# A first stage in fixed order, and three re-timings further on, in a two-layer encoder on one Trainium2 core

## The chip, the core and the metric

The kernel runs on one core of one Trainium2 chip. The core has a matrix engine (TensorE, PE in the profile; its weight loads are shown apart as PEld), a vector engine (VectorE, DVE), an engine for functions of one input (ScalarE, ACT), a general engine (GpSimd, POOL) and an engine that here issues all transfers (SyncE, SP). Each engine works through a list of instructions in the order in which they stand there; a semaphore makes an instruction wait for another engine or for a transfer, and whatever stands behind it on the same engine waits too. The metric is the device time of one execution in microseconds (us); a lower time is better.

## What is computed

The reference is an encoder of two layers over one sequence of 1024 tokens of width 1024. All arithmetic is float32.

```python
c_act = silu(c)
for l in range(2):
    mod = c_act @ ada_w[l] + ada_b[l]
    shift, scale, gate = split(mod, 3)
    h = rms_norm(x, norm_g[l]) * (1 + scale) + shift
    y = even_mixer(h) if l == 0 else odd_mixer(h)
    x = x + gate * y
return rms_norm(x, final_g)
```

`rms_norm(x, g)` is x times rstd times g, with rstd = 1 / sqrt(mean(x*x) + 1e-6) for each token. The even mixer projects h to 3072 columns, then runs differential attention (4 heads, two softmax maps each, values of width 128) and beside it a gated linear recurrence (RG-LRU) over 512 channels; both are gated and go into one output projection. The odd mixer projects h to 4096 columns, runs neighbourhood attention (16 heads, window 8 x 16 on a 16 x 64 grid), gates it and projects it back.

## The kernel before

Activations are held transposed: channels on the 128 partitions (eight blocks k = 0 to 7), tokens along the row in two halves of 512 (hf = 0, 1). To keep float32 accuracy on PE, each operand is split into a high part (type fp32r, a rounded copy) and a low part (the rest), and a product is three matmuls: high by high, high by low, low by high. Weights come in slabs of 128 output columns (512 KB). For each, ACT copies the high part (`whi`, L185) and POOL subtracts for the low part (`wlo`, L186).

**Who sets the order.** The program is written as one trace of operations. A planner then orders each engine's list by its own estimate of times: it goes by the order of the trace, but may put an operation that it takes to be ready ahead of one that it takes to be waiting. `tc.high_priority()` moves a block forward in the planner's preference. `tc.issue_after(ins)` places the block's operations that run on the engine of `ins` behind `ins` in that engine's list. SP's list is planned in the same way.

**The first stage** (L503 to L608) makes h of the first layer and the first three slabs' projections (two for the recurrence, one for the values) at once, as the transfers arrive. For each half, the squares of x are made on ACT and DVE (`squares`), summed over channels on PE (`ss_add`, L368: 32 small matmuls that leave the sums of four token groups on 32 partitions each), turned into rstd on DVE by a bit trick and three Newton steps (`rstd_rows`, eleven instructions, L378 to L384), spread over the partitions by PE (`spread`, L397) and copied to SBUF by ACT (`bcs`, L545). The modulation is made in four groups g of two channel blocks (`mod_first`): eight pieces of `ada_w` are loaded, summed on PE (L273), copied as a row by ACT (`mrow`, L296), turned by a small matmul with `pick` (L298), and DVE adds the bias (L302) and makes the gain (L304). `make_h` (L404 to L406) then makes for each k and half: x times gain times rstd on DVE, the high part with the shift on ACT, the low part on DVE. `products(i, g, hf)` (L563 to L565) adds the six matmuls of group g, slab i and half hf to the slab's PSUM bank. The sums of groups 1 to 3 stand in `high_priority` blocks, and the planner puts them well ahead of the products that need them.

**Behind the stage** a `Feed` holds projections as jobs in pieces of six matmuls, each worth 1300 credits. In the first layer's attention, each of the four `step()` calls of a unit (128 queries of a head; 33 rounds) pumps PUMP credits of such filler between the attention's own instructions. At the boundary between the layers, `out_layer` runs the output projection, half by half, eight slabs each; between its slabs the modulation of the second layer is summed: `mod_part` loads eight pieces of `ada_w`, adds them up on DVE (L334, L336), lets `wait` further turns pass, and then sums over the partitions on PE (`mrow`, L368 and L353), behind the newest projection matmul (`state["pe"]`). `NW[2]` is the number of those turns there. In the second layer, `v1_job` makes values and writes them to DRAM in eight pieces (`vd<-vt`, L1196); `load_v` reads them back in another layout (`vc<-vd`, L1208) for the products with the attention weights (L1330).

## Time and profile before

| | |
|---|---|
| median of 3 runs | 1210.18 us (1206.6 to 1210.3) |
| profiled execution, its own time | 1210.03 us |
| span of that execution's instructions | 1208.0 us |
| PE busy | 1151.2 us (95% of the span) |
| DVE, ACT, POOL busy | 728.8, 566.6, 387.0 us |
| moved by DMA | 132.26 MB |

The span runs from the first instruction to the last; the profiled execution's own time has 2.0 us more around it. An engine is busy while it executes; L numbers are lines of the kernel. `pp<-ahi,whi` names what is written and what is read, by the program's names (`ahi`, `alo` are the split activations). In a timeline row stand the start, the duration, the engine, the line, the operation, the operands and how many instructions the row merges; the bracket gives the engine's idle time ahead of it and what ended it. In a row of waits stand the instruction that waited, what it waited for, the total, how often, and the longest. The granted clock is the share of full speed that TensorE's clock was given.

### The profile page before, as it was taken

To read this page: it belongs to the slowest core of one execution; us is meant where nothing else is said; L and a number is where in the kernel's file an instruction comes from. 1 tells how busy PE (TensorE), PEld (TensorE's weight loads), DVE (VectorE), ACT (ScalarE), POOL (GpSimd) and SP (SyncE) were. 2 spreads that over 40 slices of the span, in tenths; PEclk is the share of its full clock that TensorE was granted. 3 is DMA by queue.
4 is the path that set the end of the run, shared out by engine and by line. 5 is a ranking of instruction groups with operands and counts; after the bars stand their busy time and mean duration, and the time that the engine had idled before them with its cause. 6 is when DMAs were issued, how large, how long until landed. Compare 5 with 4: busy or idle time off the path is not lost.

```text
span 1208.0 us, 19169 instructions
## 1 busy us (share of the span) xinstructions
PE 1151.2 (95%) x7232; PEld 980.0 (81%) x7232; DVE 728.8 (60%) x1414; ACT 566.6 (47%) x1031; POOL 387.0 (32%) x354
## 2 busy tenths in 40 slices
PE   4999999999999999779999899999999999999996
PEld 3788778888778887657879788988998898888896
DVE  6757949588889889658873244333444434546354
ACT  4357586466555558423433344334444434445121
POOL 2124421332323344524423332332333333216200
PEclk8999999999999999889999999999999999999998
DMA  9723132322121110276523432343445444214212
GB/s 329 228 73 122 51 94 77 94 82 75 38 86 53 58 46 21 67 231 222 179 74 117 130 93 86 94 141 101 128 132 141 136 128 132 78 52 150 99 71 71
DMA packets 82045, 132.26 MB, mean 109 GB/s; under 512 B 7584, under 2 KB 48672, under 8 KB 81952
## 3 DMA queue, kind: packets, MB, share of 16 engines
q1 hardware_dynamic: 81952, 131.03, 34.8%
q8 instruction: 57, 0.93, 0.3%
q14 instruction: 36, 0.29, 0.1%
HBM read 110.03 MB, written 14.68 MB: 103 GB/s over the span
## 4 chain that ended last, share of the span: by engine, by line
PE 78%; DVE 9%; DMA 4%; issue 4%; ACT 3%; POOL 2%; SPq 0%; DVEq 0%; POOLq 0%; ACTq 0%
PE pp L201 16%; PE pp L202 16%; PE pp L203 15%; PE no L1330 3%; PE etr L1312 3%; PE v L201 2%; PE v L202 2%; PE v L203 2%; PE atr L957 2%; DMA vd<-vt 2%; PE s L659 2%; PE s L660 2%; PE n L659 2%; PE n L660 2%; DVE e L927 1%
## 5 line engine op out<-in xcount | busy, mean ns | idle before, releaser
L202 PE MATMUL pp<-alo,whi 128*128 128x512 f32 (+1 forms) x1040 | 395.0, 380 | 3.6 <-POOL alo L226 3.6
L201 PE MATMUL pp<-ahi,whi 128*128 128x512 f32 (+1 forms) x1040 | 397.2, 382 | 0.2 <-DVE ks L630 0.2
L203 PE MATMUL pp<-ahi,wlo 128*128 128x512 f32 (+1 forms) x1040 | 394.8, 380 | 1.0 <-POOL wlo L186 1.0
L186 POOL TENSOR_TENSOR wlo<-raw,whi 128x1024 fp32r<-128x1024 f32 x80 | 197.5, 2472 | 268.5 <-ACT whi L185 254.5
L202 PEld LDWEIGHTS pp<-alo,whi 128*128 128x128 f32 x1040 | 197.1, 189 | 37.6 <-POOL alo L226 4.3
L203 PEld LDWEIGHTS pp<-ahi,wlo 128*128 128x128 f32 x1040 | 196.7, 189 | 38.1 <-POOL wlo L186 1.8
L201 PEld LDWEIGHTS pp<-ahi,whi 128*128 128x128 f32 x1040 | 196.9, 189 | 35.7 <-issue 2.1
L1301 POOL TENSOR_SCALAR e<-e,r 128x288 f32<-128x288 f32 (+1 forms) x128 | 71.3, 570 | 239.7 <-DVE r L1299 239.3
L185 ACT ACTIVATE whi<-raw 128x1024 fp32r<-128x1024 f32 x80 | 84.3, 1056 | 121.0 <-PE pp L202 65.7
L1296 ACT ACTIVATE e<-e,nm 128x288 f32<-128x288 f32 (+1 forms) x128 | 72.7, 569 | 51.3 <-DVE nm L1293 50.7
L931 ACT ACTIVATE e<-e,nm 128x1024 f32<-128x1024 f32 x64 | 73.5, 1149 | 47.7 <-DVE nm L927 45.5
L1293 DVE CUSTOM_DVE_ANT_0 e<-n,bias 128x288 f32<-128x288 f32 (+1 forms) x128 | 60.4, 504 | 51.9 <-PE n L660 32.2
L1318 DVE COPY e<-etr 96x384 f32<-96x384 f32 (+1 forms) x64 | 35.5, 554 | 91.1 <-PE etr L1312 89.5
L1316 ACT ACTIVATE e<-etr 96x384 f32<-96x384 f32 (+1 forms) x64 | 31.3, 490 | 118.9 <-DVE e L1318 118.5
L927 DVE CUSTOM_DVE_ANT_0 e<-s,tb 128x1024 f32<-128x1024 f32 x64 | 77.1, 1219 | 10.1 <-PE s L660 9.1
L201 PE MATMUL v<-whi,ahi 128*128 128x256 f32 x256 | 72.2, 282 | 0.0
L203 PE MATMUL v<-whi,alo 128*128 128x256 f32 x256 | 71.9, 281 | 0.0
L202 PE MATMUL v<-wlo,ahi 128*128 128x256 f32 x256 | 71.9, 281 | 0.0
L948 POOL TENSOR_SCALAR e<-e,r 128x256 f32<-128x256 f32 x32 | 33.9, 1059 | 110.1 <-DVE r L937 47.2
L964 ACT ACTIVATE ath<-atr 128x512 fp32r<-128x512 f32 x64 | 37.7, 596 | 40.4 <-PE atr L957 40.0
L1062 DVE SCALAR_TENSOR_TENSOR xh<-pp,mod,xh 128x512 f32<-128x512 f32 (+1 forms) x40 | 25.7, 641 | 50.8 <-PE pp L203 49.9
L1067 ACT ACTIVATE sq<-xh 128x512 f32<-128x512 f32 (+1 forms) x40 | 21.7, 543 | 72.8 <-DVE xh L1062 71.9
(207 smaller groups left out, 2076.4 us busy)
## 6 DMA issues: line engine op xcount, KB each, us to landing
raw<-in_w_dram SPq DMA_DIRECT2D x56, 512.0 KB
ada<-in_adaw_dram SPq DMA_DIRECT2D x96, 256.0 KB
raw<-in_wo_dram SPq DMA_DIRECT2D x24, 512.0 KB
bias<-in_nab_dram SPq DMA_DIRECT2D x64, 144.0 KB
qq<-qq SPq DMA_DIRECT2D x48, 128.0 KB
bias<-in_nab_dram SPq DMA_DIRECT2D x32, 192.0 KB
xT<-in_xT_dram SPq DMA_DIRECT2D x16, 256.0 KB
xh<-in_xTp_dram SPq DMA_DIRECT2D x16, 256.0 KB
```

Source lines behind the costliest of these rows:

```text
L185: A.activation(hi[:], raw[:], AF.Copy)
L186: G.tensor_tensor(lo[:], raw[:], hi[:], ALU.subtract)
L201: T.matmul(ps, lh, rh, start=start, stop=False)
L202: T.matmul(ps, lh, rl, start=False, stop=False)
L203: state["pe"] = T.matmul(ps, ll, rh, start=False, stop=stop).ins
L659: T.matmul(dst, qsel(q[m]), k, start=True, stop=False)
L660: T.matmul(dst, qsel(q[2 + m]), k, start=False, stop=True)
L927: state["dve"] = V.tensor_tensor_reduce(out=e[:], in0=ps[:].rearrange("p a b -> p (a b)"), in1=tbt[h][:, o:o + S], scale=-1.0, scalar=3.0e ...
L931: A.activation(e[:], e[:], AF.Exp, scale=-1.0, bias=nm[:], accum_out=sums[:, m:m + 1])
L1293: state["dve"] = V.tensor_tensor_reduce(out=e[:, m, :n], in0=ps[:, m, :n], in1=bias["now"][m][:, :n], scale=-1.0, scalar=3.0e38, op0=ALU.a ...
L1296: A.activation(e[:, m, :n], e[:, m, :n], AF.Exp, scale=-1.0, bias=nm[:, m:m + 1], accum_out=sums[:, m:m + 1])
L1301: state["pool"] = G.tensor_scalar(e[:, m, :n], e[:, m, :n], r[:, m:m + 1], 0.0, ALU.mult, ALU.add).ins
```

## The change

- **First stage.** A class `Pinned` wraps an engine so that each instruction issued through it stays behind everything traced on that engine so far. All squares, sums, rstd, spreads, modulation and products of the first stage go through it: the order on DVE, ACT and PE is the order of the program. `mod_first` becomes a generator in five parts (loads; sums of five pieces; sums of three; row copy; pick, bias and gain).
- rstd is a root on ACT, a reciprocal on DVE and one Newton step; the spread rstd stays in PSUM. `scaled` multiplies x by it there, ahead of the modulation; `parts` then makes the high part on ACT as x * gain + shift, the same value `h` on DVE, and the low part as `h` less the high part.
- The small constants of the recurrence are traced behind the stage, and their first DVE and ACT instructions that need the lamp load, as well as the gate weights' splits on ACT, are placed behind the stage's last `parts`.
- `PUMP` is 745 instead of 800.
- `NW[2]` is 7 instead of 3, and the rest of the second layer's modulation is stepped in the first two slabs of the boundary's second half.
- `load_v` is placed behind the newest traced write of values on SP.

```diff
-NW = (3, 3, 3, 3)
+NW = (3, 3, 7, 3)
-PUMP = 800.0
+PUMP = 745.0
...
+    class Pinned:
+        def __init__(self, eng):
+            self.eng = eng
+        def __getattr__(self, name):
+            f = getattr(self.eng, name)
+            return lambda *a, **k: tc.keep_in_program_order(f(*a, **k))
...
     def mod_first(g, pool, small, c32, V, A, T):
         pieces = []
         for k in range(KC):
...
             pieces.append(piece)
+        yield
+        ps = ptp.tile([P, HF], F32, tag="pt", name=f"mod{g}")
+        for k in range(KC):
+            for n in range(4):
+                cols = pieces[k][:, n // 2, (n % 2) * P:(n % 2 + 1) * P]
+                T.matmul(ps[32 * n:32 * n + 32, :P], c32[:, k, :], cols, start=k == 0,
+                         stop=k == KC - 1)
+            if k == 4:
+                yield
+        yield
         row = pool.tile([P, P], F32, tag="mrow", name="mrow", bufs=2)
         A.activation(row[:], ps[:, :P], AF.Copy)
+        yield
         pc = ps[:, P:]
         T.matmul(pc[:, :4], row[:], pick[:], start=True, stop=True)
...
+        def rstd(hf):
+            v, rr, t = (stp.tile([P, P], F32, tag=g, name=g)[:] for g in ("rs", "rr", "rt"))
+            pA.activation(t, nbank[hf][:, :P], AF.Sqrt, bias=eps[:], scale=1.0 / D)
+            pV.tensor_scalar(v, nbank[hf][:, :P], 1.0 / D, EPS, ALU.mult, ALU.add)
+            pV.reciprocal(rr, t)
+            pV.scalar_tensor_tensor(t, rr, -0.5, rr, ALU.mult, ALU.mult)
+            pV.tensor_tensor(t, t, v, ALU.mult)
+            pV.scalar_tensor_tensor(rr, t, 1.5, rr, ALU.add, ALU.mult)
+            return rr
+        def scaled(k, hf):
+            pV.tensor_tensor(half(k, hf), half(k, hf), nbank[hf][:], ALU.mult)
+        def parts(k, hf):
+            g, b = first_mod[k]
...
+            state["first A"] = pA.activation(hi[:], half(k, hf), AF.Identity, scale=g, bias=b).ins
+            pV.tensor_scalar(h[:], half(k, hf), g, b, ALU.mult, ALU.add)
+            state["first V"] = pV.tensor_tensor(lo[:], h[:], hi[:], ALU.subtract).ins
...
+        load_x(0)
+        mod = [mod_first(g, adp, stp, c32, pV, pA, pT) for g in range(KC // 2)]
+        next(mod[0])
         slab(0)
+        for k in range(KC):
+            square(pV if k in (2, 5) else pA, k, 0)
         with tc.issue_after(state["ada"].ins):
+            load_x(1)
+        norm_sums(0, pp, "pp")
+        next(mod[0])
+        rr = rstd(0)
+        spread(rr, nbank[0], T=pT)
+        next(mod[0])
+        scaled(0, 0)
+        scaled(1, 0)
+        square(pV, 0, 1)
+        square(pV, 1, 1)
+        next(mod[0])
         slab(1)
         with tc.issue_after(state["x"].ins):
+            next(mod[1])
+        next(mod[0])
+        parts(0, 0)
+        parts(1, 0)
+        for k in range(2, KC):
+            square(pA, k, 1)
+        for k in range(2, 6):
+            scaled(k, 0)
         products(0, 0, 0)
         products(1, 0, 0)
+        norm_sums(1, ptp, "pt")
+        rr = rstd(1)
+        spread(rr, nbank[1], T=pT)
         slab(2)
+        scaled(6, 0)
...
+        for k in (0, 1):
+            scaled(k, 1)
+        for k in (0, 1):
+            parts(k, 1)
+        scaled(7, 0)
+        products(2, 0, 0)
+        products(1, 0, 1)
+        products(0, 0, 1)
+        scaled(2, 1)
+        scaled(3, 1)
         for g in range(1, KC // 2):
+            next(mod[g])
+            next(mod[g])
+            next(mod[g])
+            products(2, g - 1, 1)
+            next(mod[g])
...
             for hf in range(2):
+                for k in (2 * g, 2 * g + 1):
+                    parts(k, hf)
+            if g == 1:
+                for k in range(4, KC):
+                    scaled(k, 1)
             for i in range(2):
                 for hf in range(2):
                     products(i, g, hf)
+            products(2, g, 0)
...
+        products(2, KC // 2 - 1, 1)
         for hf in range(2):
             evac_v(0)(hf, banks[2, hf])
+        small_constants(stp)
...
-        some(mod, 99)
         t0 = tail(0, to_h1)
         for c in range(KC):
             some(r1, 1)
+            some(mod, (4, 99)[c] if c < 2 else 0)
             some(t0, (1, 1, 2, 2, 2, 2, 0, 0)[c])
...
-            nc.sync.dma_start(vt[:4 * w], vd4[:, y, P * p:P * p + P].rearrange("g y e -> y g e"))
+            with tc.issue_after(state["vd"]):
+                nc.sync.dma_start(vt[:4 * w],
+                                  vd4[:, y, P * p:P * p + P].rearrange("g y e -> y g e"))
```

More of the change, by code (lines that the diff above doesn't have):

```diff
@@ L264, with mod_first @@
     first_mod = {}
-    def mod_first(g, pool, small, c32):
-        ps = ptp.tile([P, HF], F32, tag="pt", name=f"mod{g}")
-        def sums(x, w, start, stop):
-            for n in range(4):
-                cols = x[:, n // 2, (n % 2) * P:(n % 2 + 1) * P]
-                state["modmm"] = T.matmul(ps[32 * n:32 * n + 32, :P], w, cols,
-                                          start=start, stop=stop)
+    def mod_first(g, pool, small, c32, V, A, T):
         pieces = []
@@ L284, in mod_first @@
             pieces.append(piece)
-        if g == 0:
-            for k in range(KC):
-                sums(pieces[k], c32[:, k, :], k == 0, k == KC - 1)
-        else:
-            with tc.high_priority():
-                sums(pieces[KC - 1], c32[:, KC - 1, :], True, False)
-                with tc.issue_after(state["modmm"].ins):
-                    for k in range(KC - 1):
-                        sums(pieces[k], c32[:, k, :], False, k == KC - 2)
+        yield
[8 more added lines that the diff above has]
+        yield
         row = pool.tile([P, P], F32, tag="mrow", name="mrow", bufs=2)
         A.activation(row[:], ps[:, :P], AF.Copy)
+        yield
         pc = ps[:, P:]
@@ L364, in ss_start, with ss_add @@
         return ptp.tile([P, HF], F32, tag="pt", name=name)
-    def ss_add(ss, sq, start, stop, w=P):
+    def ss_add(ss, sq, start, stop, w=P, T=T):
         for j in range(4):
@@ L519, in squares, with square, norm_sums @@
                                                                hf * HF:(hf + 1) * HF])
+        def square(eng, k, hf):
+            sq = sqs[k, hf] = stp.tile([P, HF], F32, tag="sq", name="sq", bufs=SQ)
+            if eng is pV:
+                pV.tensor_tensor(sq[:], half(k, hf), half(k, hf), ALU.mult)
+            else:
+                pA.activation(sq[:], half(k, hf), AF.Square)
+        def norm_sums(hf, pool, tag):
             ss = nbank[hf] = pool.tile([P, HF], F32, tag=tag, name=f"norm{hf}")
-            sqs = []
@@ L537 @@
-        bcs = {}
-        def scale(hf):
-            with tc.high_priority():
-                rr = rstd_rows(nbank[hf], D, stp)
-                spread(rr, nbank[hf])
-                bcs[hf] = stp.tile([P, HF], F32, tag="bcs", name="bcs")
-                A.activation(bcs[hf][:], nbank[hf][:], AF.Copy)
-        def parts(g, hf):
-            for k in (2 * g, 2 * g + 1):
-                make_h(0, k, hf, half(k, hf), bcs[hf][:])
+                ss_add(ss, sqs[k, hf], k == 0, k == KC - 1, T=pT)
@@ L562, in products @@
                 ps, (wh, wl), (hi, lo) = banks[i, hf], ready[i], hact[k, hf]
[L563 to L568 removed]
+                pT.matmul(ps, wh[:, k, :], hi[:], start=k == 0, stop=False)
+                pT.matmul(ps, wl[:, k, :], hi[:], start=False, stop=False)
@@ L577 @@
         products(0, 0, 0)
         products(1, 0, 0)
+        norm_sums(1, ptp, "pt")
+        rr = rstd(1)
+        spread(rr, nbank[1], T=pT)
         slab(2)
-        with tc.issue_after(state["modmm"].ins):
-            scale(1)
-        parts(0, 1)
-        with tc.issue_after(state["x"].ins):
-            mod_first(2, adp, stp, c32)
-        for i in range(2):
-            products(i, 0, 1)
-        rest = [(2, 0, 0), (2, 0, 1)]
-        for g in range(1, KC // 2):
+        scaled(6, 0)
+        with tc.issue_after(state["ada"].ins):
+            next(mod[2])
@@ L590 @@
+        for k in (0, 1):
[8 more added lines that the diff above has]
+        scaled(3, 1)
+        for g in range(1, KC // 2):
+            next(mod[g])
[3 more added lines that the diff above has]
+            next(mod[g])
             if g == 1:
-                with tc.issue_after(state["x"].ins):
-                    mod_first(3, adp, stp, c32)
+                with tc.issue_after(state["ada"].ins):
+                    next(mod[3])
@@ L597 @@
                     products(i, g, hf)
-            for args in rest:
-                products(*args)
-            rest = [(2, g, 0), (2, g, 1)]
+            products(2, g, 0)
         for i, evac in enumerate((evac_xb(0), evac_xb(1))):
@@ L603 @@
                 evac(hf, banks[i, hf])
-        for args in rest:
-            products(*args)
+        products(2, KC // 2 - 1, 1)
         for hf in range(2):
             evac_v(0)(hf, banks[2, hf])
+        small_constants(stp)
         ahead(3)
@@ L821 @@
         vj = lambda h: both(at0[c_v + h], evac_v(h))
-        gate_w(0)
-        gate_w(1)
+        with tc.issue_after(state["first A"]):
+            gate_w(0)
+            gate_w(1)
         kq0 = lambda: chain(both(at0[c_k], evac_k(("a", 0))), both(at0[c_q], evac_q(("a", 0))))
```

53 lines of the change are left out of this document (19 added, 34 removed).

## The prediction

> **What bounds the kernel now.** I read the page's busy line first, then the waits of TensorE (PE), then windows around each wait, and last the timeline of the first stage, whose every instruction is re-ordered.
>
> ```profile
> span 1208.0 us, 19169 instructions
> PE 1151.2 (95%) x7232; PEld 980.0 (81%) x7232; DVE 728.8 (60%) x1414; ACT 566.6 (47%) x1031; POOL 387.0 (32%) x354
> ```
>
> PE is idle for 56.8 us of the span; PE work itself hardly changes, so the change can only move idle time and half clock. The waits of PE, longest first (total, times, longest):
>
> ```profile
> PE norm L368 <- ACT sq L527: 7.9, 2, 6.9
> PE mrow L368 <- issue: 7.3, 1, 7.3
> PE start L563 <- ACT ahi L405: 6.1, 2, 4.1
> PE no L1330 <- DMA vc<-vd: 4.2, 3, 3.4
> PE pp L202 <- POOL alo L226: 3.6, 2, 3.2
> PE obc L397 <- DVE osq L384: 3.3, 2, 2.6
> ```
>
> Four places: the first stage (norm, start), the tail of the first layer's attention (alo, obc), the boundary between the layers (mrow), and the value loads of the second layer (vc). Windows around them (busy of PE, PEld, DVE, ACT, POOL, then granted clock, DMA share, GB/s):
>
> ```profile
> 39.00:75.00 36.00, 35.77 (x261) 28.92 (x262) 24.73 (x34) 16.73 (x25) 7.20 (x3) 0.95 0.38 120
> ...
> 228.00:464.00 236.00, 232.69 (x1392) 193.49 (x1391) 205.59 (x418) 141.28 (x248) 80.08 (x80) 1.00 0.20 62
> 464.00:516.00 52.00, 43.58 (x252) 35.65 (x251) 38.33 (x71) 30.00 (x45) 26.04 (x20) 0.90 0.13 41
> ...
> 527.00:542.00 15.00, 7.66 (x28) 5.53 (x27) 7.29 (x11) 2.59 (x4) 2.82 (x2) 0.66 0.89 296
> ...
> 682.00:692.00 10.00, 6.60 (x61) 5.52 (x60) 3.40 (x8) 3.13 (x6) 3.33 (x3) 0.83 0.61 179
> ```
>
> Two things to see. The late first stage (39 to 75) has only 0.2 us of idle PE. And a wait costs twice: at 682 to 692 PE idles 3.4 us, and a clock of 0.83 over 10 us is 3.4 us at half, 1.7 us more.
>
> **Part 1, the first stage.** The rows that carry it:
>
> ```profile
> 0.80 1.28 ACT L258 ACT_TABLE_LOAD   x1 [0.80 <-PEq L1479]
> ...
> 14.47 0.29 DVE L378 TENSOR_SCALAR rs<-norm 128x128 f32<-128x128 f32 x1
> ...
> 17.67 0.29 DVE L384 SCALAR_TENSOR_TENSOR rr<-rt,rr 128x128 f32<-128x128 f32 x1
> ...
> 21.94 2.34 POOL L186 TENSOR_TENSOR wlo<-raw,whi 128x1024 fp32r<-128x1024 f32 x1 [12.52 <-ACT whi L185]
> 21.98 3.50 DVE L404 SCALAR_TENSOR_TENSOR xT<-xT,gain,bcs 128x512 f32<-128x512 f32 x2
> ...
> 24.86 1.39 ACT L405 ACTIVATE ahi<-xT,first 128x512 fp32r<-128x512 f32 x2 [3.00 <-DVE xT L404]
> ...
> 25.63 0.79 PE L563 MATMUL start<-ahi,whi 128*128 128x512 f32 x1 [4.08 <-ACT ahi L405]
> ...
> 30.39 1.95 PE L368 MATMUL norm<-sq,ones 128*32 128x128 f32 x64
> ...
> 33.85 1.96 PE L273 MATMUL mod<-ada,c 128*32 128x128 f32 x64
> ```
>
> ```profile
> L334 DVE TENSOR_SCALAR macc<-ada,ctmp 128x512 f32<-128x512 f32 x8 | 3.8, 480 | 0.0
> ...
> L525 DVE TENSOR_TENSOR sq<-xT 128x512 f32<-128x512 f32 x5 | 3.3, 684 | 0.0
> ...
> L392 DVE RECIPROCAL rr<-rs 128x128 f32<-128x128 f32 x1 | 1.0, 953 | 0.3 <-ACT rs L391 0.3
> ```
>
> *Head start.* The eleven-instruction rstd lasts from 14.47 to 17.96, 3.5 us. Root, reciprocal and three steps are 0.29 (as the 128x128 read of the sums at 14.47) + 0.95 + 3 x 0.33 (3.5 us over eleven) = 2.2 us. A new ACT table load (1.28 us in the first row) may stand before the root; so a half saves 0 to 1.3, and I take 1.2 for the second, where the load has already happened. On the first half the saving is lost: the fixed DVE order puts two squares of x's second half ahead of the modulation's gain, and they need its second piece, some 5.8 MB down the queue.
>
> ```profile
> 0.00:19.20 19.20, 7.31 (x116) 5.29 (x118) 13.46 (x62) 6.60 (x11) 4.29 (x11) 1.00 0.90 304
> ```
>
> 304 GB/s x 19.2 us = 5.8 MB, so it lands between 19.2 and 20.2; squares and gain end near 21.3 (now 21.95). But the multiply that the POOL split stretches (3.50 us for two at 21.98) is off the path: `hi` comes straight from ACT, and the first product starts near 22.2, not 25.63. Most of the 3.4 us is given back: the first `lo` still needs DVE behind the same 2.3 us of POOL, and the twelve products run at half clock (twice the 0.23 us quoted below) to 29; the second half's sums end near 31.2 instead of 32.3. With the shorter rstd (1.2) less what the second half's `lo` costs (it needs three DVE instructions now, not two), I take **-2.1** at the point where 30 products and the sums of group 1 are done. Ends: -4 (full clock from 26 us) and 0 (the table load and POOL take it all).
>
> *Stall per group.* The sums of groups 1 to 3 now stand on PE directly before their group, and nothing else follows their pick but products that need that gain. Now they stand early (33.85), which is why 39 to 75 has no idle.
>
> ```profile
> 46.37 0.34 PE L298 MATMUL mod<-pick,mrow 128*128 128x4 f32 x2
> ...
> 46.94 0.16 DVE L304 SCALAR_TENSOR_TENSOR gain<-first,sm 128x2 f32<-128x2 f32 x1
> ...
> 47.93 2.05 ACT L405 ACTIVATE ahi<-xT,first 128x512 fp32r<-128x512 f32 x3 [1.66 <-DVE xT L404]
> ```
>
> ```profile
> 47.04 0.23 PE start L565
> ```
>
> Pick ends 46.71, gain 47.10: 0.4 us. Then `hi` 0.7 on ACT and `lo` 0.68 on DVE: the first pair is ready 1.5 us after the gain. Each further pair costs DVE 0.48 (h) + 0.68 (lo) less some 0.06 of overlap, 1.1 us, where PE uses 3 x 0.23 = 0.7. Four pairs: 0.4 + 1.5 + 3 x 1.1 + 0.23 = 5.4 us, holding 12 x 0.23 = 2.7 of products: 2.7 us idle per group, **+8.2** for three. Low end: h hides behind other work and a pair costs 0.6, 1.2 per group, +3.6. High end: the clock halves too, 1.7 each (the price read at 682), +13.
>
> The stage so ends 6.1 us later, at 80.5 instead of 74.42:
>
> ```profile
> 65.09 0.60 ACT L415 ACTIVATE xb<-start 128x512 f32<-128x512 f32 x1 [5.05 <-PE start L565]
> ...
> 74.42 0.39 PE L201 MATMUL pp<-ahi,whi 128*128 128x512 f32 x1
> ```
>
> The first bank is now emptied at 65.09, later only 24 products (5.4 us) before the end, at 75: the convolutions start 10 us later. Three projections, 16 us, cover that; if the cover fails it costs the 4 us by which 10 exceeds 6. Small constants and gate weights cost nothing: small DVE, ACT and POOL work beside a busy PE; with no cover, one more 1.28 us table load.
>
> **Part 2, thinner filler.** The feed holds 19 projections of four pieces, 1300 credits each: 98,800. At 800 a step they last 123.5 of the 132 steps, at 745 they last 132.6. So 124 x 55 ns = 6.8 us of products move to the last two units, where PE idles 8.4 us (464 to 516) and a clock of 0.90 over 52 us loses another 5.2: at most -13.6. That the units get shorter needs PE to set them: 98.6% against 87% of DVE in 228 to 464 says so. But the order there is the planner's, and the next layer's splits (alo) mix in; I take just under half, **-6**; ends -13.6 and +6.8 (rival C).
>
> **Part 3, later sums.** The first part's sums move two projections (2 x 24 x 0.23 = 11 us) down PE's queue, past the wait of 7.3 us; with the clock of 0.66 (10.2 us at half, 7.1 of them worked, 3.2 lost) at most -10.5. Late next is the weight slab after the one PE then takes:
>
> ```profile
> 532.62 0.38 SPq L156 DMA_DIRECT2D raw<-in_wo_dram  x1
> ...
> 538.41 1.06 ACT L185 ACTIVATE whi<-raw 128x1024 fp32r<-128x1024 f32 x1 [2.57 <-DMA raw<-in_wo_dram]
> ```
>
> ```profile
> 539.54 2.37 POOL L186 TENSOR_TENSOR wlo<-raw,whi 128x1024 fp32r<-128x1024 f32 x1 [12.09 <-ACT whi L185]
> ```
>
> Its low part is ready at 541.9; PE gets there near 544 now. If that load stays where it is, the gain is 2.2 us. The second part's ada loads start four calls later, which relieves queues that are 0.89 busy: **-5**, ends -2.2 and -10.5.
>
> **Part 4, value loads.** SP's queue:
>
> ```profile
> 670.15 0.34 SPq L1208 DMA_DIRECT2D vc<-vd  x1
> 670.53 0.49 SPq L1196 DMA_DIRECT2D vd<-vt  x1
> 675.62 0.39 SPq L1208 DMA_DIRECT2D vc<-vd  x1
> ...
> 677.06 0.50 SPq L1196 DMA_DIRECT2D vd<-vt  x1
> ...
> 683.61 1.45 SPq L1208 DMA_DIRECT2D vc<-vd  x3
> ```
>
> A load waits for the landing of the write ahead of it (4.6 us from 671.02, the end of the issue at 670.53, to 675.62) and holds back the write behind it. With the writes first (the last at about 671), the loads issue near 676, nearly 8 us earlier, and the wait of 3.4 us and its 1.7 of half clock go, and most of the other 0.8: **-5.5**; ends -5.9 and 0 (the weight and bias loads queued behind the loads become late).
>
> **Sum.** +6.1 - 6 - 5 - 5.5 = -10.4 on the profiled execution's 1210.03 us (2.0 over its span, 0.15 under the median 1210.18): **1199.6 us**.
>
> **Rivals.** *A, the fixed order gains as well:* stalls at their low end and head start at its high end, stage -0.4, total -16.9: 1193. For it: DVE waits often while POOL splits run, and POOL is nearly free in 39 to 75. Against: four pairs still pass one DVE. *B, waits at the seams move instead of going:* tail 0, sums -2.2, values -5.5, stage +6.1: 1208.4. For it: queues 0.89 busy, splits on POOL. *C, slower: the filler covered DVE.* If units keep their length, the 6.8 us of products are added at the end: +6.1 + 6.8 - 2.2 - 5.5, 1215.2. It decides once PE's idle in 228 to 464, now 3.3 us, passes 10. Against it the 98.6%. *D, the stalls halve the clock* in all three groups: 3 x 1.7 more, 1204.7. For it 682 to 692; against it, each stall is in pieces under 1.3 us. The Trainium skill's page "TensorE: Matmul & The Clock Gate" (section "A second HAM failure mode: psum-queue depth-cycling") says that frequent micro-idles between groups make the gate oscillate. By that rule D holds; 39 to 75, with a clock of 0.95 and no such pieces, cannot test it.
>
> **How the numbers follow.** Forecast 0.37, A 0.22, B 0.16, C 0.15, D 0.10. Under 0.3% (3.6 us) a measurement of this kernel cannot tell from no change. Faster: the forecast, A and D but for their upper edges, 0.64; same: B and those edges, 0.20; slower: C and a little of B, 0.16. Range 1188 (A with more of the tail) to 1215 (C's value). The likeliest case's own is 1194 to 1206.
>
> **What would show it.** Stage: the first projection's first matmul after 78 and a PE wait on `ahi` or `alo` behind each pick (right), or at 74 or earlier (A). Tail: idle under 4 us in the attention's last 50 us; in the units before, under 6 us (else C). Boundary: no `mrow` wait, and whether PE waits on a slab's `wlo` instead. Values: writes in one row on SP, no wait on `vc`. A total above 1206 would prove the forecast wrong.

## The result, and the profile after

The changed kernel takes 1214.44 us (median of 6 runs, 1213.13 to 1215.65), the kernel before 1208.86 us (6 runs, 1206.6 to 1210.3). The ratio is 1.0046, interval 1.0031 to 1.0061: slower, where the forecast was 10 us faster. The profiled execution took 1213.13 us.

First the page's span and busy line of the kernel after. PE does the same work (1153.4 us busy, 1151.2 before); it is idle 1.2 us more, and the other 2.2 us of the longer span lie in its busy time, with the same 7232 matmuls.

```profile
span 1211.4 us, 19204 instructions
PE 1153.4 (95%) x7232; PEld 976.6 (81%) x7232; DVE 729.5 (60%) x1417; ACT 570.2 (47%) x1034; POOL 384.9 (32%) x354
```

PE's waits in the kernel after (what waited and for what, total, times, longest):

```profile
PE start L208 <- ACT ahi L208: 8.6, 5, 4.4
...
PE obc L402 <- DVE osq L389: 7.2, 3, 5.1
PE start L208 <- DVE alo L208: 4.1, 11, 1.3
PE norm L208 <- DVE rr L208: 2.9, 2, 2.7
PE pp L213 <- POOL wlo L186: 2.8, 2, 1.7
...
PE gate L211 <- ACT xch L764: 2.2, 1, 2.2
```

Against the list of before: `mrow` (7.3) and `vc` (4.2) are gone; new are `start <- alo`, eleven times, `norm <- rr`, `gate <- xch`, and a slab's `wlo` at the boundary. `obc` has grown from 3.3 to 7.2.

Windows of the kernel after (busy of PE, PEld, DVE, ACT, POOL, granted clock, DMA share, GB/s): the late first stage, the attention's units, their last stretch with the tail, and the place of the value loads.

```profile
39.00:88.00 49.00, 40.80 (x328) 28.84 (x328) 22.72 (x44) 16.78 (x26) 6.10 (x3) 1.00 0.29 94
244.00:480.00 236.00, 230.50 (x1380) 192.55 (x1379) 205.89 (x422) 139.48 (x246) 76.72 (x78) 0.99 0.20 60
480.00:528.00 48.00, 40.71 (x247) 33.60 (x246) 39.47 (x67) 32.48 (x47) 28.75 (x21) 0.93 0.14 45
...
692.00:702.00 10.00, 10.00 (x88) 8.78 (x87) 4.71 (x11) 3.91 (x9) 3.71 (x4) 1.00 0.52 160
```

The late first stage was full before (0.2 us of idle PE in 39 to 75); now it has 8.2 us of idle PE, at full clock. The stretch with the tail has 7.3 us of idle PE in 48, hardly less than the 8.4 in 52 before. The value loads' window was 66% busy at a clock of 0.83; now it is full.

To see where the time went, I cut every trace at the same events: the first `pp` matmul (end of the stage), the first logit matmul `s<-ks,qq` of the attention, the last of them, the last `obc` (end of the attention's tail), the first logit matmul `n<-ks,qq` of the second layer, and the 49th product with values `no<-e,vc`. The table has the length of each stretch in us; the rows below the first two are the experiments. One profiled execution each, so a stretch whose work is the same still differs: the stage of the kernel before ends between 71.96 and 74.42 in the six traces that have it unchanged, and its tail lasts 29 or 31.7.

| kernel | stage | recurrent part | units | tail | boundary | first values | rest | span |
|---|---|---|---|---|---|---|---|---|
| before | 74.4 | 152.9 | 256.9 | 31.7 | 127.1 | 72.3 | 492.7 | 1208.0 |
| after | 87.1 | 156.7 | 250.6 | 33.3 | 124.9 | 67.1 | 491.7 | 1211.4 |
| stage alone | 87.5 | 156.2 | 256.9 | 29.0 | 126.9 | 71.1 | 493.1 | 1220.5 |
| three seams alone | 74.3 | 154.3 | 250.9 | 33.4 | 125.7 | 66.9 | 491.8 | 1197.3 |
| early sums | 74.9 | 153.1 | 250.7 | 33.4 | 125.0 | 67.0 | 491.7 | 1195.8 |
| squares on ACT | 87.8 | 156.6 | 251.0 | 33.3 | 123.7 | 67.0 | 492.2 | 1211.6 |
| both | 76.9 | 154.6 | 251.0 | 33.4 | 127.0 | 67.0 | 491.7 | 1201.5 |
| filler alone | 72.0 | 152.5 | 251.4 | 33.4 | 127.9 | 71.4 | 492.9 | 1201.5 |
| sums alone | 73.9 | 152.5 | 256.9 | 31.7 | 126.2 | 70.5 | 493.8 | 1205.5 |
| value loads alone | 72.0 | 152.6 | 256.0 | 29.2 | 127.6 | 67.2 | 490.9 | 1195.4 |
| filler and sums | 72.5 | 152.4 | 252.1 | 33.4 | 125.5 | 73.3 | 494.3 | 1203.5 |
| seams, root | 73.2 | 154.3 | 251.3 | 33.4 | 125.3 | 66.9 | 492.2 | 1196.6 |
| h on ACT | 84.0 | 156.5 | 251.3 | 33.4 | 123.2 | 67.0 | 491.8 | 1207.1 |
| early sums, late squares | 75.0 | 153.1 | 251.4 | 33.4 | 128.0 | 66.9 | 491.4 | 1199.2 |

The two first rows give the whole: stage +12.7, recurrent part +3.8, units -6.2, tail +1.6, boundary -2.3, values -5.2, rest -1.0; sum +3.4 us of span.

How the stage loses, in three views of the kernel after. Its start (DVE, then POOL, then PE rows in order of time):

```profile
20.68 3.51 DVE L208 TENSOR_TENSOR sq<-xT 128x512 f32<-128x512 f32 x2 [0.87 <-DMA xT<-in_xT_dram]
...
24.29 0.16 DVE L208 SCALAR_TENSOR_TENSOR gain<-first,sm 128x2 f32<-128x2 f32 x1
```

```profile
21.30 2.34 POOL L186 TENSOR_TENSOR wlo<-raw,whi 128x1024 fp32r<-128x1024 f32 x1 [11.42 <-ACT whi L185]
```

```profile
25.35 0.79 PE L208 MATMUL start<-ahi,whi 128*128 128x512 f32 x1 [4.45 <-ACT ahi L208]
...
35.53 1.16 PE L208 MATMUL norm<-rr,sel 128*128 128x128 f32 x8 [2.66 <-DVE rr L208]
```

Two squares stand on DVE ahead of the first gain. Alone they take 0.69 us each; beside POOL's split, which lasts from 21.30 to 23.64, the pair ends only at 24.19, and the gain is there at 24.45. So the first product starts at 25.35, 0.3 us before the old one. The Trainium skill's page "SBUF — State Buffer" (section "Who interferes with whom") says that a DVE instruction with two SBUF inputs and a GpSimd instruction that reads SBUF block one another; these rows agree. Then PE stands still for 2.66 us while the second half's root, reciprocal and Newton step run.

Then each group. PE's rows behind the pick of group 1, and DVE's for one pair of high and low parts:

```profile
46.23 0.28 PE L208 MATMUL mod<-pick,mrow 128*128 128x4 f32 x2
47.80 0.50 PE L208 MATMUL start<-ahi,whi 128*128 128x512 f32 x1 [1.30 <-ACT ahi L208]
...
49.78 0.50 PE L208 MATMUL start<-alo,whi 128*128 128x512 f32 x1 [0.29 <-DVE alo L208]
...
52.30 0.50 PE L208 MATMUL start<-alo,whi 128*128 128x512 f32 x1 [0.29 <-DVE alo L208]
52.64 0.40 PE L208 MATMUL start<-ahi,whi 128*128 128x512 f32 x1
```

```profile
48.40 0.54 DVE L208 TENSOR_SCALAR h<-xT,gain,first 128x512 f32<-128x512 f32 x1
49.04 0.69 DVE L208 TENSOR_TENSOR alo<-h,ahi 128x512 fp32r<-128x512 f32 x1
49.65 0.54 DVE L208 TENSOR_SCALAR h<-xT,gain,first 128x512 f32<-128x512 f32 x1
```

From the pick's end (46.51) to 52.64 are 6.1 us with twelve products of 0.23: 3.4 us lost. The waits for `alo` (three of them) come 1.26 us apart, DVE's time for a pair (48.40 to 49.65). Group 2 looks the same; group 3 loses one more microsecond, explained below.

Last, the recurrent part's start in the kernel after. ACT:

```profile
78.36 0.60 ACT L420 ACTIVATE xb<-start 128x512 f32<-128x512 f32 x1
...
82.84 0.58 ACT L420 ACTIVATE xb<-start 128x512 f32<-128x512 f32 x1
83.43 1.28 ACT L507 ACT_TABLE_LOAD   x1
...
85.79 1.06 ACT L420 ACTIVATE xb<-start 128x512 f32<-128x512 f32 x2
86.74 1.24 ACT L751 ACTIVATE xc<-xb,sm 128x1024 f32<-128x1024 f32 x1
```

ACT before:

```profile
67.47 0.58 ACT L415 ACTIVATE xb<-start 128x512 f32<-128x512 f32 x1
68.08 1.25 ACT L699 ACTIVATE xc<-xb,sm 128x1024 f32<-128x1024 f32 x1
```

and PE in the kernel after:

```profile
94.86 0.50 PE L211 MATMUL gate<-xch,gwh 128*128 128x512 f32 x1 [2.17 <-ACT xch L764]
...
95.90 0.62 PE L211 MATMUL pp<-ahi,whi 128*128 128x512 f32 x1
```

The first bank is emptied 13.3 us later than before (65.09), little more than the 12.7 us by which the whole stage ends later. But the convolution (`xc`), which needs both halves, starts 18.7 us later. Before, it followed the second half's bank at once; now a table load, an Exp, a copy of a weight slab's high part and two more banks, 3.3 us together, stand between them in ACT's list. On PE one projection of 24 products stands ahead of the first gate, now (87.09 to 92.5) as before (74.42 to 79.86). It runs out, and PE waits 2.2 us for the convolution's result; then its matmuls stand 0.43 us apart instead of 0.23 from 95.9 to 99.3 (eight of them), 1.6 us more.

### The profile page after: what moved, and what is told of

It is laid out like the page before. It is cut to its first block, busy times and chain, and to the rows that moved or that the text cites. A ratio compares the mean times of both kernels' runs of the same rounds, so it can differ in the third digit from the quotient of the medians.

```text
span 1211.4 us, 19204 instructions
## 1 busy us (share of the span) xinstructions
PE 1153.4 (95%) x7232; PEld 976.6 (81%) x7232; DVE 729.5 (60%) x1417; ACT 570.2 (47%) x1034; POOL 384.9 (32%) x354
## 4 chain that ended last, share of the span: by engine, by line
PE 76%; DVE 11%; ACT 4%; DMA 4%; issue 2%; POOL 1%; SPq 0%; DVEq 0%; ACTq 0%; POOLq 0%
PE pp L211 15%; PE pp L212 15%; PE pp L213 15%; PE no L1386 3%; PE etr L1368 3%; PE v L211 2%; PE v L213 2%; PE v L212 2%; PE start L208 2%; PE n L711 2%; PE atr L1010 2%; DVE e L980 2%; PE n L712 2%; PE s L711 2%; PE s L712 1%
## 5 line engine op out<-in xcount | busy, mean ns | idle before, releaser
L1357 POOL TENSOR_SCALAR e<-e,r 128x288 f32<-128x288 f32 (+1 forms) x128 | 71.1, 568 | 232.3 <-DVE r L1355 231.9
L1120 ACT ACTIVATE sq<-xh 128x512 f32<-128x512 f32 (+1 forms) x40 | 21.8, 544 | 72.5 <-DVE xh L1115 71.7
L711 PE MATMUL s<-ks,qq 128*128 128x512 f32 x128 | 52.8, 413 | 2.5 <-DVE nm L980 2.5
## 6 DMA issues: line engine op xcount, KB each, us to landing
ada<-in_adaw_dram SPq DMA_DIRECT2D x96, 256.0 KB
qq<-qq SPq DMA_DIRECT2D x48, 128.0 KB
xT<-in_xT_dram SPq DMA_DIRECT2D x16, 256.0 KB
xh<-in_xTp_dram SPq DMA_DIRECT2D x16, 256.0 KB
```

The costliest lines, as they stand in the source:

```text
L711: T.matmul(dst, qsel(q[m]), k, start=True, stop=False)
L1357: state["pool"] = G.tensor_scalar(e[:, m, :n], e[:, m, :n], r[:, m:m + 1], 0.0, ALU.mult, ALU.add).ins
```

## The experiments

Differences in us below are the ratio's distance from 1, with its interval, times 1208. My theory after the comparison was: the stage alone makes the loss, because nothing on PE covers the way from a pick to its group's parts; the seams gain separately. The rivals stand in the expectations.

**The stage alone.** The changed kernel with filler, sums and value loads as before.

```diff
-NW = (3, 3, 7, 3)
+NW = (3, 3, 3, 3)
...
-PUMP = 745.0
+PUMP = 800.0
...
+        some(mod, 99)
...
-            some(mod, (4, 99)[c] if c < 2 else 0)
...
-            with tc.issue_after(state["vd"]):
```

> The changed kernel with its three other parts undone (filler 800 again, sums of the modulation back in front of the tail, value loads without the wait for the writes). Theory 1 (the first stage alone makes the loss: its end 12.7 us later, the recurrent part 3.8 more): first gate matmul near 95, whole kernel 16 to 17 us over the kernel before, 1225, ratio 1.013 to 1.014. Theory 2 (the parts disturb one another: the later stage shifts the planner's order, and the thinner filler or the moved sums lose what they should bring): the stage alone costs about the 6.1 us of the forecast, 1215, and its end is nearer 80 than 87.

Measured: 1223.49 us, ratio 1.0126 (1.0104 to 1.0149), +15.2 us (12.6 to 18.0). Stage end 87.5, recurrent part 156.2. Theory 1: the stage costs what the comparison shows, and the later stage doesn't change the units (256.9).

**The seams alone.** The kernel before with the other three parts.

```diff
-NW = (3, 3, 3, 3)
+NW = (3, 3, 7, 3)
...
-PUMP = 800.0
+PUMP = 745.0
...
-        some(mod, 99)
...
+            some(mod, (4, 99)[c] if c < 2 else 0)
...
+            with tc.issue_after(state["vd"]):
```

> The kernel before with filler 745, the sums moved into the tail and the value loads behind the writes; the first stage as it was. Theory 1: the three seams keep what the comparison of the two traces shows for them (4.6 + 2.2 + 5.2 and up to 2 more): 12 to 14 us under the kernel before, 1195 to 1197. Theory 2: with the early start of the recurrent part the order is another and the gains are not these; the sum of the three is 5 us or less, 1204 or above.

Measured: 1196.36 us, ratio 0.9899 (0.9878 to 0.9920), -12.2 us (-14.7 to -9.7). Theory 1 again; +15.2 and -12.2 make +3.0, the whole change measured +5.6 (3.7 to 7.4). The two halves are about independent.

**Early sums.** The changed kernel in its fixed order, but the sums of groups 1 to 3 one group earlier, those of group 1 in the 2.66 us of the second rstd. Behind the picks of groups 2 and 3 now stand 18 products that need no new gain, behind that of group 1 six.

```diff
         rr = rstd(1)
+        next(mod[1])
+        next(mod[1])
+        next(mod[1])
         spread(rr, nbank[1], T=pT)
...
+        next(mod[1])
+        products(2, 0, 1)
         for g in range(1, KC // 2):
-            next(mod[g])
-            next(mod[g])
-            next(mod[g])
-            products(2, g - 1, 1)
-            next(mod[g])
...
-            for i in range(2):
-                for hf in range(2):
-                    products(i, g, hf)
-            products(2, g, 0)
+            products(0, g, 0)
+            products(0, g, 1)
+            if g < KC // 2 - 1:
+                for _ in range(3):
+                    next(mod[g + 1])
+            products(1, g, 0)
+            if g < KC // 2 - 1:
+                next(mod[g + 1])
+            products(1, g, 1)
+            products(2, g, 0)
+            if g < KC // 2 - 1:
+                products(2, g, 1)
```

> The changed kernel, its fixed order kept, but the sums of groups 1 to 3 stand one group earlier on PE, and the pick with 18 products (4.1 us) behind it that don't need the new gain; the sums of group 1 stand in the 2.7 us in which PE waits for the root and Newton step of the second half. Theory 1 (the loss is that nothing on PE covers the gain and the four pairs on VectorE): no idle time behind the picks, 10 us less there and up to 2.7 at the second rstd, first layer's first gate matmul 12 us or more earlier than in the changed kernel, 1199 to 1203. Theory 2 (VectorE's pace of 1.25 us a pair bounds the groups wherever the sums stand): PE idles as long, only at other products; 1210 or above. Theory 3 (the late emptying of the first bank is a cost by itself): the stage ends 12 us earlier but the recurrent part keeps its 3.8 us.

Measured: 1198.34 us, ratio 0.9919 (0.9898 to 0.9941), -9.8 us against the kernel before and some 15 under the changed one. The late stage in this kernel:

```profile
39.00:75.00 36.00, 34.67 (x257) 26.43 (x257) 23.68 (x44) 16.88 (x25) 5.32 (x3) 1.00 0.33 104
```

and PE's rows behind the pick of group 3:

```profile
62.01 0.28 PE L208 MATMUL mod<-pick,mrow 128*128 128x4 f32 x2
62.15 0.48 PE L208 MATMUL start<-ahi,whi 128*128 128x512 f32 x1
```

No idle time follows the picks of groups 2 and 3; the stage ends at 74.88 instead of 87.09. Theory 1: DVE still needs 1.25 us a pair, but 4.1 us of products run meanwhile. Group 1 is a smaller test in the same run: with six products (1.4 us) behind its pick, PE still waits three times 0.29 us for `alo`, and 2.2 us are lost (41.75 to 48.10 with eighteen products of 0.23) instead of 3.4. Of the 12.2 us by which the stage is shorter, 3.1 are there when 30 products and the sums of group 1 are done (41.61 instead of 44.71): 2.0 because these sums fill the second rstd's wait, the rest because the first twelve products left half clock sooner in this execution (25.24 to 29.86, there 25.35 to 30.87). 9.1 come behind that point, in the groups.

Theories 2 and 3 fall: the recurrent part is back at 153.1 with no wait at the gate (first gate 5.5 us behind the stage's end), though the extra ACT table load is still there. ACT's rows say why it no longer costs anything:

```profile
68.52 1.28 ACT L507 ACT_TABLE_LOAD   x1
...
70.87 0.58 ACT L420 ACTIVATE xb<-start 128x512 f32<-128x512 f32 x1
71.48 1.25 ACT L758 ACTIVATE xc<-xb,sm 128x1024 f32<-128x1024 f32 x1
```

The second half's bank is emptied about as far ahead of the stage's end as in the changed kernel (4.0 us, there 4.3), and PE has the same 24 products ahead of the gate. But the table load now stands ahead of that bank, in time in which ACT waited (2.9 us ahead of 81.87 in the changed kernel), and the convolution follows at once. So the rows point to the 3.3 us in ACT's list, and not to the late stage by itself; no run changed that list alone. And this stage ends no earlier than the old one: the fixed order, the shorter rstd and the product ahead of the gain, once their damage is undone, gain nothing that I can see.

**Squares on ACT.** The changed kernel, with no square of the second half on DVE.

```diff
-        square(pV, 0, 1)
-        square(pV, 1, 1)
...
-        for k in range(2, KC):
+        for k in range(KC):
             square(pA, k, 1)
```

> The changed kernel with the two squares of the second half, which VectorE does ahead of the first gain, given to ScalarE behind the first two parts. Theory 1 (these two squares, 3.5 us beside a GpSimd split, hold the first gain back): first gain near 21.5 instead of 24.4, first product near 22.5 instead of 25.35, the whole 1 to 3 us less, since the products then still run at half clock and the sums of the second half follow later. Theory 2 (the stage from its second half on is set by the loads of x and by ScalarE): first product earlier, the stage end at 87 as before, no difference.

Measured: 1213.42 us, ratio 1.0037 (1.0021 to 1.0053), the changed kernel's time. PE in this kernel:

```profile
22.08 0.50 PE L208 MATMUL start<-ahi,whi 128*128 128x512 f32 x1 [2.80 <-ACT ahi L208]
...
35.86 1.57 PE L208 MATMUL norm<-rr,sel 128*128 128x128 f32 x8 [4.66 <-DVE rr L208]
```

The first product starts 3.3 us earlier, as the forecast had it (near 22.2). PE then waits 1.6 us for the first low part and 4.66 instead of 2.66 us for the second rstd. The time is theory 2's. One row of DVE and one of POOL show what took the gain away:

```profile
32.86 2.29 DVE L208 SCALAR_TENSOR_TENSOR rt<-rr 128x128 f32<-128x128 f32 x1
```

```profile
32.66 2.34 POOL L186 TENSOR_TENSOR wlo<-raw,whi 128x1024 fp32r<-128x1024 f32 x1 [8.89 <-ACT whi L185]
```

The second half's sums are done at 31.19 instead of 32.88. But one instruction of the Newton step takes 2.29 us instead of 0.29, beside the POOL split of the third slab, which here runs later: ACT copied the slab's high part behind the root (31.54) instead of ahead of it (29.03). So 2.0 us are lost to a meeting of DVE and POOL, and the run does not show what an earlier start is worth without it.

**Both.** The two rearrangements together.

> The changed kernel with both rearrangements: sums of groups 1 to 3 one group earlier, and all squares of the second half on ScalarE. Theory 1 (with the sums early, the first products set the stage, so the earlier first gain now counts): stage end 1 to 3 us under the 74.9 of the kernel with early sums alone, whole kernel 1195 to 1197. Theory 2 (the second half's squares and its rstd set the start of the middle of the stage, whatever comes first): stage end 74.9 or later, 1198 to 1200.

Measured: 1202.03 us, ratio 0.9961 (0.9948 to 0.9975). That is worse than early sums alone (their intervals don't meet). A miss of theory 1, and a little worse than theory 2; the second spread comes at 36.51 instead of 34.47. The squares are not late: the second half's sums are done at 31.85, with early sums at 31.82. The same Newton instruction takes 2.29 us again, beside the POOL split at 33.31, and that is the 2.0 us.

**Early sums, late squares.** The kernel with early sums, and DVE's two squares moved behind the first two parts.

```diff
-        square(pV, 0, 1)
-        square(pV, 1, 1)
...
         parts(1, 0)
+        square(pV, 0, 1)
+        square(pV, 1, 1)
```

> The kernel with the sums of groups 1 to 3 one group earlier, and VectorE's two squares of the second half moved behind the first two parts, so that the first gain doesn't wait for them; ScalarE keeps its six. Theory 1 (the start of the products sets the stage): first product at 22 to 22.5 instead of 25.2, stage end 1 to 3 us under 74.9, whole kernel 1195.5 to 1197.5. Theory 2 (the rstd of the second half, which needs all eight squares, sets it): first product as early, but PE idle as much longer before the second spread, the whole as with early sums, 1197.5 to 1200.

Measured: 1198.98 us, ratio 0.9939 (0.9919 to 0.9960); early sums had 0.9919. The first product starts 4.5 us earlier, and the stage ends at the same time. PE in this kernel:

```profile
20.69 0.50 PE L208 MATMUL start<-ahi,whi 128*128 128x512 f32 x1 [1.40 <-ACT ahi L208]
...
30.33 0.43 PE L208 MATMUL mod<-ada,c 128*32 128x128 f32 x8 [0.33 <-DMA ada<-in_adaw_dram]
...
32.58 0.42 PE L208 MATMUL mod<-ada,c 128*32 128x128 f32 x8 [0.31 <-DMA ada<-in_adaw_dram]
33.65 2.07 PE L208 MATMUL norm<-rr,sel 128*128 128x128 f32 x8 [0.64 <-DVE rr L208]
```

Now the sums of group 1 wait for their pieces of `ada_w`, which land one every 0.75 us (262 KB each, 350 GB/s), the last near 32.6. Behind them PE waits 0.64 us more, for the second rstd, in which the same instruction meets a POOL split (at 30.45) for the third time:

```profile
30.64 2.30 DVE L208 SCALAR_TENSOR_TENSOR rt<-rr 128x128 f32<-128x128 f32 x1
```

By my estimate (the rstd's end at 33.59 less the 2.0 us) the rstd would have been there near 31.6, ahead of the last piece. So the transfers and the POOL split both hold PE near 33 us, and from 31 to 37 the granted clock is 0.72, with early sums 1.00. Theory 2's outcome: the rstd does come last, but not because of its squares. In both kernels the pick of group 1 starts near 41.7.

**h on ACT.** The changed kernel, with every second `h` of groups 1 to 3 on ACT.

```diff
-            pV.tensor_scalar(h[:], half(k, hf), g, b, ALU.mult, ALU.add)
+            if k % 2 and k > 1:
+                pA.activation(h[:], half(k, hf), AF.Identity, scale=g, bias=b)
+            else:
+                pV.tensor_scalar(h[:], half(k, hf), g, b, ALU.mult, ALU.add)
```

> The changed kernel with h of every odd channel group beyond the first pair made by ScalarE, so that VectorE has 0.65 us for that pair and 1.25 for the other. Theory 1 (VectorE's pace over the four pairs sets the time from pick to sums): each of the three groups 1 us or more shorter, stage end 3 to 4 us earlier, 84, whole kernel 1209 to 1211. Theory 2 (ScalarE's pace, the pick and the gain set it): no difference, 1213 to 1215.

Measured: 1211.35 us, ratio 1.0033 (1.0016 to 1.0051): not told apart from the changed kernel. The stage ends 3.1 us earlier, but 1.4 of that is there at the pick of group 1, ahead of the edit; from pick to pick it is 13.76 us instead of 14.0, so a group gains 0.25, not 1. The last group gains 1.2, since its `h` no longer meets the split of the gate weights on POOL (explained below). DVE in this kernel shows why the groups gain so little:

```profile
47.81 0.69 DVE L208 TENSOR_TENSOR alo<-h,ahi 128x512 fp32r<-128x512 f32 x1 [0.72 <-ACT h L208]
```

DVE now waits for ACT, which makes a high part and an `h` in 1.4 us. The bound moved from one engine to the next. The stage's end is theory 1's (84), but the groups did not shorten as it said, and the whole time lies between the two theories. Of these two edits only cover on PE took the loss away; a pair that is made faster was not run.

**The seams one by one**, on the kernel before: filler alone, sums alone, value loads alone, then filler and sums together (each with its lines of the diff above).

> The kernel before with the filler at 745 instead of 800 and nothing else. Theory 1 (the thinner filler alone shortens the attention's tail): 4 to 6 us less, 1203 to 1204. Theory 2 (the filler's gain in the changed kernel came from the later stage having shifted the planner's order): within 2 us of the kernel before. Theory 3 (the idle time goes from the tail into the units, or part of it comes back at the boundary, where the layer's last products now meet the mrow wait): attention 4 to 6 us shorter, but the mrow wait longer, total 2 us or less.

> The kernel before with the sums of the modulation moved into the tail and nothing else. Theory 1 (the wait of 7.3 us for the row of the modulation goes, but the next slab is late): no mrow wait, waits on a slab's two parts of some 3 us in its place, 2 us less in all, 1206. Theory 2 (the boundary loses all of its 7.3 us and its half clock when the slab isn't late): 1198 to 1200. Theory 3 (the wait is hidden anyway): the time of before.

> The kernel before with the value loads issued behind the writes and nothing else. Theory 1 (the three waits on vc and the half clock behind the first go): 5 to 7 us less, 1201 to 1203. Theory 2 (the loads are late elsewhere, since they now stand behind the last write): a wait on bias or on later values takes their place, 3 us or less.

> The kernel before with the filler at 745 and the sums of the modulation in the tail; value loads as they were. Theory 1 (the two need one another: with either alone the idle time at the boundary is taken up by the next late thing, the row of the modulation, 4.6 us, or the next weight slab, 6.3 us; together only 3.5 us of waits for the slab are left): boundary 125 to 126 us long instead of 127 to 128, whole kernel 4 to 8 us under the kernel before, 1200 to 1203. Theory 2 (the gains add up singly, about 1 us and nothing): 1206 to 1207, and the value loads alone make what all three together gain.

| | us | ratio, interval | difference |
|---|---|---|---|
| filler alone | 1205.97 | 0.9992 (0.9978 to 1.0005) | -1.0 |
| sums alone | 1208.19 | 1.0006 (0.9988 to 1.0024) | +0.7 |
| value loads alone | 1200.95 | 0.9957 (0.9942 to 0.9973) | -5.2 |
| filler and sums | 1204.01 | 0.9968 (0.9949 to 0.9986) | -3.9 |

The value loads bring their 5.2 us alone. Filler and sums bring nothing that can be told alone, and some 4 us together, just short of what theory 1 of the last expectation wanted. By its interval the filler alone may still bring up to 2.7 us, so the times alone do not prove that the two need one another; the traces below speak for it. The value loads and the pair add up to -9.1 us, and all three seams measured -12.2 (-14.7 to -9.7); where the other 3 us come from is open. With the filler alone, PE's waits still have

```profile
PE mrow L368 <- issue: 4.6, 1, 4.6
```

and with the sums alone the wait changes its name. The two rows are the last `obc` of the tail and the next long wait on PE, first with the sums alone, then with all three seams:

```profile
513.86 1.16 PE L397 MATMUL obc<-osq,sel 128*128 128x128 f32 x8
...
538.33 0.79 PE L201 MATMUL pp<-ahi,whi 128*128 128x512 f32 x1 [6.27 <-ACT whi L185]
```

```profile
511.74 1.16 PE L397 MATMUL obc<-osq,sel 128*128 128x128 f32 x8
...
535.77 0.50 PE L201 MATMUL pp<-ahi,whi 128*128 128x512 f32 x1 [1.76 <-ACT whi L185]
```

The slab's high part is there 23 us after the `obc` in both (538.33 - 515.02; 535.77 - 512.90). But with filler 745, PE comes to it 21.1 us after the `obc` instead of 17.0: the thinner filler leaves 4 us of products over, and they are worked off behind the tail, where they cover the late slab. With the sums alone the idle time only changes from `mrow` to `whi`; with the filler alone the 4 us of products cover part of the `mrow` wait.

**Seams with the root.** The three seams on the kernel before, and rstd of the first stage by root and one Newton step, in the planner's order.

```diff
-                rr = rstd_rows(nbank[hf], D, stp)
+                v, rr, t = (stp.tile([P, P], F32, tag=g, name=g)[:] for g in ("rs", "rr", "rt"))
+                A.activation(t, nbank[hf][:, :P], AF.Sqrt, bias=eps[:], scale=1.0 / D)
+                V.tensor_scalar(v, nbank[hf][:, :P], 1.0 / D, EPS, ALU.mult, ALU.add)
+                V.reciprocal(rr, t)
+                V.scalar_tensor_tensor(t, rr, -0.5, rr, ALU.mult, ALU.mult)
+                V.tensor_tensor(t, t, v, ALU.mult)
+                V.scalar_tensor_tensor(rr, t, 1.5, rr, ALU.add, ALU.mult)
```

> The kernel before with the three seams and, in the first stage, rstd by root, reciprocal and one Newton step in place of the eleven instructions; order left to the planner. Theory 1 (the shorter rstd counts where the order isn't fixed, since the first product waits for ScalarE behind VectorE behind rstd): stage end 1 to 2.5 us earlier, whole kernel 1193 to 1195.5. Theory 2 (the second half's loads and a table load set the start, the rstd is covered): as with the seams alone, 1196 to 1198.

Measured: 1198.87 us, ratio 0.9932 (0.9909 to 0.9955); the seams alone had 0.9899 (0.9878 to 0.9920). No gain: theory 2, a little above its range. The rstd is 1 us shorter (2.5 instead of 3.5), and again the sums of group 1 wait for `ada_w` at 32.84.

The best versions are the seams on the old stage (1196.4) and the changed kernel with early sums (1198.3); their intervals overlap.

## Why the prediction was wrong

By stretch, the forecast's -10.4 became +3.4 of span, 13.8 us apart. Of these, 10.4 lie in the first part of the change.

- **Head start: -2.1 forecast, +0.8 measured.** By the equal point (30 products and the sums of group 1 done) the changed kernel is at 44.71, the old one at 43.91. Single executions differ here by 2 us (41.5 to 43.9 in the six traces of the old stage; 43.6 for the new one in the stage-alone kernel), so only the missing gain is sure. The step that failed: "squares and gain end near 21.3"; they ended at 24.45. I had the squares beside the POOL split and priced them as if free of it, although I quoted, a sentence later, the 3.50 us that the same split made of two multiplies. What the term left out is the 2.66 us of idle PE at the second rstd, where the old order ran the sums of group 1. The range's end of 0 was too tight. With these sums early, the same point is reached at 41.6 and 41.7 (early sums; early sums, late squares), at the early end of the old stage's spread; a head start that lasts to the end of the stage appears in no run.
- **Stall per group: +8.2 forecast, +11.2 measured.** The mechanism was right, and early sums bear it out: with the cover back the groups are 9.1 us shorter, and the 2.2 us still lost stand where the cover is 1.4 us. The size was off: I let `h` and `lo` overlap (1.1 us a pair, measured 1.25), and the first matmul behind a wait takes longer. That makes 3.4 a group instead of 2.7. One more microsecond is in group 3, where an `h` met a POOL split. DVE and POOL in the kernel after:

```profile
78.93 1.51 DVE L208 TENSOR_SCALAR h<-xT,gain,first 128x512 f32<-128x512 f32 x1
```

```profile
78.49 1.66 POOL L780 TENSOR_TENSOR gwl<-gwr,gwh 128x512 fp32r<-128x512 f32 x1 [45.98 <-ACT gwh L779]
```

  This is the gate weights' split that I costed at nothing "beside a busy PE": here DVE was on the path. 12.0 of the stage's 12.7 us are so accounted for; 0.7 are not.
- **The cover of the recurrent part: 0 forecast, +3.8 measured.** Two steps failed. "The convolutions start 10 us later": they start 18.7 us later, 6.0 more than the stage ends later, and 3.3 of these are the work ahead of them in ACT's list, of which I had named only the table load, and put it at nothing. "Three projections, 16 us, cover that": one projection, 5.4 us, stands ahead of the first gate, before and after. "It costs the 4 us" came near the measured price by luck, from the wrong 10 less 6; and I left it out of the sum. Early sums give the 3.8 us back.
- **Thinner filler: -6 forecast; units and tail -4.6 in the trace, -1.0 alone.** The units shortened by 6, so rival C's condition (over 10 us of idle PE in them) was not met: 5.5. But the products did not move into the tail's idle time, which the step said; the tail lasts 33.3 or 33.4 us in every kernel with 745, with the same 5.1 us wait for `osq`. My test for the tail, idle under 4 us, was not met (7.3): the wait for `alo` (3.6) is gone, and that for `osq` has grown by 3.9. The products moved behind it, to the boundary.
- **Later sums: -5 forecast, -2.3 in the trace, nothing alone.** What I had as the low bound came out: PE waits for the slab, its `whi` and then its `wlo`, instead of `mrow`. I had named "late next" rightly and then took a value between the bounds for a relief of queues that the trace does not show. (The half clock's price of 3.2 us in that working is 3.6 by its own figures, 7.1 us worked at half; only the far end changes.)
- **Value loads: -5.5 forecast, -5.2 in that stretch and -5.2 alone.** Right, with the mechanism: in SP's rows of the kernel after the last write goes ahead of the loads, and no wait for `vc` is left.

```profile
681.80 0.49 SPq L1249 DMA_DIRECT2D vd<-vt  x1
682.39 0.93 SPq L1263 DMA_DIRECT2D vc<-vd  x2
```

The total fell where rival C put it (1215.2), but not by C. Rival D (the stalls halve the clock) was wrong: over 39 to 88 the granted clock is 1.00 and equal matmuls stand 0.23 us apart, with idle pieces of 0.3 to 1.3 us in each group. The Trainium skill's "TensorE: Matmul & The Clock Gate" (section "A second HAM failure mode: psum-queue depth-cycling") describes a kernel whose micro-idles made the clock oscillate; here such pieces, 14 us apart as sets of four, did not. Of the prediction's own tests, the total above 1206 said that the forecast was wrong; the first projection after 78, the `ahi` and `alo` waits behind each pick and a slab's `wlo` in place of `mrow` came out, and the tail's idle time did not.

The error behind most of it is one: in the old stage the sums of each group stood early, and I priced their loss too low, and everything that followed a late stage by zero.

## What to carry to other kernels

When an order is fixed by hand, look at each small result that a group of work needs (here a gain of 256 numbers) and count what the engine can do between its request and its use; with 4.1 us of other products behind the pick the same chain cost nothing, with 1.4 us of them 2.2 us, without them 3.4. When a step makes a chain later, put the next chain's cover into the sum as a term and check it, since its price is already known. When work moves earlier, look at what it now runs beside: in three kernels the rstd came 2 us late because one short instruction on DVE met a weight split on POOL. Two seams can need one another: where removing a wait only brings the next late thing forward, work left over from elsewhere is what turns it into time.

## What the runs showed of the hardware

- Two squares of 0.69 us each took 3.51 us beside a POOL subtraction of 2.34; an instruction of 0.29 us on 128x128, both inputs the SBUF tile `rr`, took 2.29 or 2.30 beside one of 2.34 in three kernels; and an `h` (one SBUF tensor and two columns in, SBUF out) 1.51 instead of 0.54 beside one of 1.66. The last ended 0.3 us after POOL's end at 80.15, less than its own 0.54 us; spans on POOL are rough, so this does not show that the two overlapped.
- Idle pieces of up to 1.3 us on PE, in sets 14 us apart, left equal matmuls at 0.23 us; so did the 2.66 us ahead of 35.53, while the 2.2 us at the gate were followed by 3.4 us of matmuls at 0.43. With early sums and late squares, waits of 0.3 to 0.6 us between 30 and 33.65 were followed by a spread of 2.07 us instead of 1.16, and the granted clock from 31 to 37 was 0.72. Neither the length of a wait nor its being short tells by itself whether it is paid twice.
- The pieces of `ada_w` landed at 350 GB/s until about 32.6 us; the two kernels whose sums of group 1 were ready ahead of that (early sums with late squares; seams with the root) waited for them.
- In the kernel after, the row of the granted clock says 1.00 for 24 to 31, while its first twelve products stand 0.43 us apart there; the distance of equal matmuls was the surer sign.
